# Small clipped subtractions on GpSimd, a later triangle selection, and padded tiles in a two-layer retention and delta-rule encoder

## The chip, the cores and the metric

The kernel runs on one core of one Trainium2 chip. The metric is the device time in microseconds of one execution. Three timed runs of the kernel before gave 1135.25 us as the median (1132.84, 1135.25 and 1136.71). A separate execution was profiled; the trace comes from that one.

The engines are named as in the profile: PE is the matrix engine, PEld its weight loads, DVE the vector engine, ACT the scalar engine, POOL is GpSimd, and SP issues nearly all transfers. L215 is line 215 of the kernel before.

## What is computed

Two layers, each with a token mixer and a feed-forward part, on a (256, 1024) float32 matrix. The parts that the change touches belong to the gated delta rule, which runs forwards and backwards over two chunks of 128 tokens, for eight heads:

```
h = rmsnorm(x);  one projection of h gives all mixer inputs and gates
gc   = cumsum(g) within a chunk                    # g < 0, so gc falls along the chunk
diff = gc[i] - gc[j]
dec  = exp(where(i >= j, diff, -inf))              # decays: 0 above the diagonal
A    = beta * (k k^T) * dec, strictly below the diagonal
solve (I + A) u = beta v                           # in blocks of 32, then 64, then 128
attn = (q k^T) * dec, diagonal included
o    = decayed q times the state + attn times (u - ...)
x    = x + W_out( gate_a * P_ret(retention) + gate_b * P_dn(delta rule) )
x    = x + W2( relu(rmsnorm(x) W1)^2 )
```

## The kernel before, in words

**Products.** Every large product is done in three parts, since a float32 operand is split in a high part and a low part: high times high, high times low, low times high. A weight tile of 128 x 1024 numbers (`wraw`, 512 KB) is loaded by SP, its high part `whi` is made by ACT (L180) and its low part `wlo` by DVE (L181). There are three buffers of each. Two helpers use them. `chan_pair` (L202) makes channel-major outputs: the weight block stays in the array and the 256 tokens are streamed, so each product has 256 columns (L215 to L217). `tok_chunk` (L184) makes token-major outputs: the tokens stay and 512 weight columns are streamed (L197 to L199). The streamed tokens are `hTh`/`hTl` (the transposed, normalized input), `h2h`/`h2l` for the feed-forward part, and `yrh`/`yrl`, `ydh`/`ydl` for the two merge projections. The names of the outputs in the profile: `pcd` (delta-rule inputs), `pcrq` (retention queries and keys), `parv`, `parg` (retention values and gates), `padz`, `pcga`, `pcgb` (gates), `pcpr`, `pcpd` (merge projections), `pawo` (output projection), `pcf` and `paf` (the two feed-forward products).

**Where tiles lie.** Pools are laid out one behind the other in a partition, a tile at its size. The weight buffers come first, each 4096 bytes; behind them the two halves of `x` (tag `x0`, `x1`), then `hTh0`, `hTh1`, `hTl0`, `hTl1`, then small tiles, then the tiles of the mixer, which hold `yrh` and its like. All sizes from the first weight buffer to `hTl1` are multiples of 4096 bytes (two buffers for small projections share a slot), so `hTh`, `hTl` and the weight parts begin at the same place modulo 4096.

**Decays.** For each layer, `gates_small` (L249) makes `gc`, writes its transpose to `rowd` and reads it back into the decay tiles `E` with every row repeated over the 128 partitions (L327). There are two halves of heads (`hf`), each with two directions `d`, so four pieces of 128 x 1024 numbers a layer. POOL subtracts `gc` from a whole piece (L330, a tensor of columns broadcast along the rows) and then sets everything on the wrong side of the diagonal to -1e30 (L334, an affine selection). ACT takes the exponential of a half at a time (L341), which makes those places 0. The buffers of the later block solve, `W` (L338), `D` (L498) and `DT` (L505), are set to zero by POOL.

**Delta rule.** `half_inputs` (L371) projects keys and queries of a half, passes them through a convolution of five taps (L358 to L364, on ACT and DVE) and transposes them. The sums of squares `ssq` go to POOL for a power of -0.5 (`rs`, L130 called from L395); `sA` (L404, L405) is made from it. `delta_kk` (L434) multiplies the products `ps_kk` by `sA` and `E` into `A` (L448) and by `E` alone into `E` itself (L450, the attention weights), all on DVE; then diagonal blocks of 32 go through memory to `delta_solve` (L463), which starts with X = -Gm and ones on the diagonal (L468, L469) and runs 30 steps of two DVE operations (L474, L476). X and its transpose `XT` go to memory and come back in 40 small transfers for `delta_levels` (L484; products `ps_y` L515, `ps_m` L525, `ps_mt` L532), and then follows `delta_out` (L563).

**Order.** The body is written as generators for retention and delta rule, interleaved by the string `SEQ` (L59). A scheduler then orders each engine's instructions, with priorities for weight loads and splits, and that order is fixed when the program runs: an engine whose next instruction waits does nothing else. At the start of a layer `normed` (L133) waits for POOL as well: the power `r` (L130) of the mean square is taken there, for each of the two token tiles, before DVE can scale `x` (`xn`, L145) and PE can transpose it (`pstn`, L167).

Of the kernel before, what the change touches and what calls it, by code (L numbers as in the profile page):

```python
# [8 lines left out]
F32 = mybir.dt.float32  # L9
F32R = mybir.dt.float32r  # L10
AF = mybir.ActivationFunctionType
ALU = mybir.AluOpType
AX = mybir.AxisListType

P = 128
D = 1024
S = 256
DEPTH = 2
NT = S // P
# [4 lines left out]
HH = 4  # L24
CK = 5
# [10 lines left out]
def tile_trunk(ctx, tc, x, norm1_g, w_in, conv_w, a_log, dt_bias, ret_gn_g, dn_norm_g,  # L36
# [3 lines left out]
    V, A, G, T = nc.vector, nc.scalar, nc.gpsimd, nc.tensor  # L40

    def pool(name, bufs, space=None, c=ctx):
        kw = {} if space is None else {"space": space}
        return c.enter_context(tc.tile_pool(name=name, bufs=bufs, **kw))

    cst = pool("cst", 1)
    wp = pool("wp", 3)
    hp = pool("hp", 1)
# [9 lines left out]

    SEQ = "11111011101101"  # L59

    xh = [hp.tile([P, NT, 512], F32, tag=f"x{j}", name=f"x{j}") for j in range(2)]
    cc = cst.tile([P, C_END - C_GAM], F32, tag="cc", name="cc")
    prow = sm.tile([P, 4, P], F32, tag="junk", name="prow")
    rows1, rows2, crow = prow[:16, 0], prow[:34, 1], [prow[:CK * 24, 2 + l] for l in range(DEPTH)]
# [40 lines left out]

    gT = cst.tile([P, 16], F32, tag="gT", name="gT")
    gT2 = cst.tile([P, 34], F32, tag="gT2", name="gT2")
    cw = [cst.tile([P, CK * 24], F32, tag=f"cw{l}", name=f"cw{l}") for l in range(DEPTH)]

    def columns(dst, src, n):  # L110
        ps = aux.tile([P, 512], F32, tag="aux", name="ps_g")
# [106 lines left out]
        return ps  # L218

    def halves(tag, p, nm, dt=F32R):  # L220
        return [p.tile([P, 4, S], dt, tag=f"{tag}{j}", name=f"{nm}{j}") for j in range(2)]

    hT_hi, hT_lo = None, None
    for l in range(DEPTH):
# [24 lines left out]
        def gates_small():  # L249
# [6 lines left out]
            for k in range(KT):  # L256
                a, b = hT_hi[k // 4][:, k % 4, :], hT_lo[k // 4][:, k % 4, :]
# [4 lines left out]
            with tc.high_priority(offset=300):  # L262
# [30 lines left out]
                p = s16("spp")  # L293
# [16 lines left out]
                gc = gx[:, 0]  # L310
# [12 lines left out]
            for hf in range(2):  # L323
                for d in range(2):
                    E = Es[hf][:, d]
                    for c in range(NT):
                        DQ.dma_start(  # L327
                            E[:, c], rowd[d, c, d, HH * hf:HH * hf + HH, :].partition_broadcast(P))
                    i0 = 8 * d + HH * hf
                    G.tensor_tensor(E, E, gc[:, :, i0:i0 + HH].unsqueeze(3).broadcast_to([P, NT, HH, P]),  # L330
                                    ALU.subtract)
                    ev = E.rearrange("p c h i -> p (c h) i")
                    sg = 1 if d == 0 else -1
                    G.affine_select(ev, ev, pattern=[[0, 8], [sg, P]], base=0, channel_multiplier=-sg,  # L334
                                    compare_op=ALU.is_ge, fill=-1e30)
            Ws = [dl.tile([P, 8, P], F32, tag="W", name="W", bufs=2) for hf in range(2)]
            for hf in range(2):
                G.memset(Ws[hf], 0.0)  # L338
# [95 lines left out]
        def delta_kk(hf, q):  # L434

            kq, sA = q["kq"], q["sA"]
            E = [sc["E"][hf][:, d] for d in range(2)]
            Am = [dl.tile([P, NT, HH, P], F32, tag=f"A{d}", name=f"A{d}", bufs=2) for d in range(2)]
            for c in range(NT):
                cs = slice(c * P, (c + 1) * P)  # L440
                for i in range(2):
                    ps = dps.tile([P, 2, 2, P], F32, tag="dps", name="ps_kk")
                    for e in range(2):
                        T.matmul(ps[:, e], lhsT=kq[i][:, e, 0, cs], rhs=kq[i][:, e, :, cs], start=True, stop=True)
                    for d in range(2):
                        for e in range(2):
                            h = 2 * i + e
                            V.scalar_tensor_tensor(Am[d][:, c, h, :], ps[:, e, 0, :], sA[:, d, c, h:h + 1],  # L448
                                                   E[d][:, c, h, :], ALU.mult, ALU.mult)
                        V.tensor_tensor(E[d][:, c, 2 * i:2 * i + 2, :], ps[:, :, 1, :],  # L450
                                        E[d][:, c, 2 * i:2 * i + 2, :], ALU.mult)
            adg = sm.tile([P, 16, 32], F32, tag="junk", name="adg")
            Av = [a.rearrange("p c h i -> p (c h) i") for a in Am]
            for b in range(4):
                bs = slice(32 * b, 32 * b + 32)
                A.activation(adg[bs, 0:8, :], Av[0][bs, :, bs], AF.Copy)
                V.transpose(adg[bs, 8:16, :], Av[1][bs, :, bs])
            for d, b, c in PAIRS:
                G.tensor_copy(sc["W"][hf][blk[b], :, blk[c]], Av[d][blk[b], :, blk[c]])
            DQ.dma_start(sc["gd"][64 * hf:64 * hf + 64].rearrange("(u b) (j i) -> (b j) u i", b=4, i=32), adg)  # L460
            q.update(E=E, Av=Av)

        def delta_solve():  # L463

            Gm = dl.tile([P, 32, 32], F32, tag="G", name="Gm")
            DQ.dma_start(Gm, sc["gd"].rearrange("q (j i) -> q j i", i=32))
            X = dl.tile([P, 32, 32], F32, tag="X", name="X")
            V.tensor_scalar(X, Gm, -1.0, None, ALU.mult)  # L468
            V.memset(X.rearrange("p a b -> p (a b)")[:, 0:1024:33], 1.0)  # L469
            for j in range(1, 31):  # L470
                n = 31 - j
                tm = sm.tile([P, 256], F32, tag="stm", name="stm", bufs=1)
# [319 lines left out]
        for i in range(4):  # L792
            ps = chan_pair(w_proj_dn[l][:, 256 * i:256 * (i + 1)], yTh, yTl, "pd")
            for e in range(2):
                k = 2 * (i % 2) + e
# [5 lines left out]
        xh = [hp.tile([P, NT, 512], F32, tag=f"x{j}", name=f"x{j}") for j in range(2)]  # L801
# [23 lines left out]
        for i in range(16):  # L825
            ps = chan_pair(w_ff1[l][:, 256 * i:256 * (i + 1)], hT_hi, hT_lo, "f1")
            for e in range(2):
                k = 2 * i + e
# [82 lines left out]
```

## Time and profile before

| | us |
|---|---|
| median of three timed runs | 1135.25 |
| profiled execution, its own time | 1128.0 |
| its span, first to last instruction | 1126.3 |
| PE busy | 1082.3 |
| PEld busy | 1003.9 |
| DVE busy | 765.7 |
| ACT busy | 599.5 |
| POOL busy | 195.2 |

The mean granted clock of PE is 0.982 of full speed. Busy times of PE are modelled and overlap with each other, so the spacing of the starts of products says more than the length of one. The stages in the profiled execution, by its timeline: layer 0 has its mixer first, the feed-forward products from 384 us on, and ends at 566 us; layer 1 follows in the same way. POOL begins on the decays at 63 us and at 620 us, and the block solve runs from 150 to 202 us and from 706 to 758 us.

### The profile page before, as it was taken

Reading aid. Unit: us, or ns where it says so; the run is one execution under the profiler, and the core shown is the slowest. Engines: PE = TensorE matmul, PEld = TensorE weight load, DVE = VectorE, ACT = ScalarE, POOL = GpSimd, SP = SyncE. Lnnn points to the kernel's source line nnn. Section 1 sums busy time; section 2 is a strip of 40 time slices with the busy share of each in tenths; the row PEclk is TensorE's granted clock in tenths of the full one; section 3 lists DMA queues with packets and bytes.
Section 4 is the critical chain, followed back from the end, with each engine's and each line's share of the span. In section 5 each row is a group of like instructions: output and inputs, shape, how many; then the busy total and the mean of one; then the engine's idle time right before and its main releaser. Section 6 shows DMA issues by size and latency. Waiting matters only on the chain. (4 is left out here: it accounts for less than half of the span.)

```text
span 1126.3 us, 19629 instructions
## 1 busy us (share of the span) xinstructions
PE 1082.3 (96%) x7564; PEld 1003.9 (89%) x7564; DVE 765.7 (68%) x1359; ACT 599.5 (53%) x1046; POOL 195.2 (17%) x193
## 2 busy tenths in 40 slices
PE   6988999999999999999989899999999999999997
PEld 5988888989999899988879898989999989999885
DVE  4998999646576666644468898994657566666453
ACT  5986654433364566533359865454334556555342
POOL 2065200100002043300020751001001012332000
PEclk9999999989999999999999899999999999999999
DMA  6565675453545466556556556655444565655662
GB/s 211 160 182 157 173 211 150 114 158 97 153 145 183 157 203 182 177 191 211 171 165 177 161 162 193 187 154 135 124 142 113 173 204 165 192 185 188 188 194 104
DMA packets 175759, 188.43 MB, mean 167 GB/s; under 512 B 36240, under 2 KB 137010, under 8 KB 175666
## 3 DMA queue, kind: packets, MB, share of 16 engines
q1 hardware_dynamic: 174288, 185.17, 55.0%
q10 hardware_dynamic: 1378, 2.02, 0.5%
q8 instruction: 59, 0.97, 0.4%
q14 instruction: 34, 0.28, 0.1%
HBM read 181.85 MB, written 5.31 MB: 166 GB/s over the span
## 5 line engine op out<-in xcount | busy, mean ns | idle before, releaser
L181 DVE TENSOR_TENSOR wlo<-wrawc,whi 128x1024 fp32r<-128x1024 f32 x192 | 240.7, 1254 | 117.3 <-ACT whi L180 113.3
L180 ACT ACTIVATE whi<-wrawc 128x1024 fp32r<-128x1024 f32 x192 | 202.7, 1057 | 150.0 <-PE pcpr L216 25.3
L181 DVE TENSOR_TENSOR wlo<-wraw,whi 128x1024 fp32r<-128x1024 f32 x128 | 158.2, 1236 | 111.7 <-ACT whi L180 111.6
L180 ACT ACTIVATE whi<-wraw 128x1024 fp32r<-128x1024 f32 x128 | 135.5, 1059 | 172.3 <-PE paf L199 92.0
L216 PE MATMUL pcf<-h2l,whi 128*128 128x256 f32 x512 | 143.8, 283 | 0.0
L217 PE MATMUL pcf<-h2h,wlo 128*128 128x256 f32 x512 | 143.0, 283 | 0.0
L215 PE MATMUL pcf<-h2h,whi 128*128 128x256 f32 x512 | 142.0, 284 | 0.0
L217 PE MATMUL pcd<-hTh,wlo 128*128 128x256 f32 x384 | 110.8, 292 | 0.9 <-DVE wlo L181 0.9
L215 PE MATMUL pcd<-hTh,whi 128*128 128x256 f32 x384 | 110.3, 291 | 0.0
L216 PE MATMUL pcd<-hTl,whi 128*128 128x256 f32 x384 | 109.8, 287 | 0.0
L199 PE MATMUL paf<-whi,fl 128*128 128x512 f32 x256 | 100.8, 394 | 0.0
L198 PE MATMUL paf<-wlo,fh 128*128 128x512 f32 x256 | 100.7, 394 | 0.0
L216 PEld LDWEIGHTS pcf<-h2l,whi 128*128 128x128 f32 x512 | 98.2, 192 | 0.0
L217 PEld LDWEIGHTS pcf<-h2h,wlo 128*128 128x128 f32 x512 | 98.0, 192 | 0.0
L215 PEld LDWEIGHTS pcf<-h2h,whi 128*128 128x128 f32 x512 | 97.1, 192 | 0.0
L197 PE MATMUL paf<-whi,fh 128*128 128x512 f32 x256 | 90.2, 392 | 0.0
L832 POOL TENSOR_TENSOR fz<-fz 128x256 f32<-128x256 f32 x64 | 66.6, 1042 | 117.7 <-ACT fz L831 116.7
L215 PEld LDWEIGHTS pcd<-hTh,whi 128*128 128x128 f32 x384 | 73.9, 194 | 1.1 <-issue 0.2
L217 PEld LDWEIGHTS pcd<-hTh,wlo 128*128 128x128 f32 x384 | 73.5, 193 | 1.6 <-DVE wlo L181 1.2
L216 PEld LDWEIGHTS pcd<-hTl,whi 128*128 128x128 f32 x384 | 74.1, 193 | 0.4
L363 DVE SCALAR_TENSOR_TENSOR cacc<-pcd,cw,cacc 128x255 f32<-128x255 f32 (+1 forms) x144 | 67.1, 475 | 5.7 <-ACT cac L359 4.7
L197 PEld LDWEIGHTS paf<-whi,fh 128*128 128x128 f32 x256 | 48.1, 188 | 11.0
(268 smaller groups left out, 2637.6 us busy)
## 6 DMA issues: line engine op xcount, KB each, us to landing
wrawc<-in_w_in_dram SPq DMA_DIRECT2D x96, 512.0 KB, 3.8
wrawc<-in_w_ff_dram SPq DMA_DIRECT2D x64, 512.0 KB, 3.7
wraw<-in_w_ff_dram SPq DMA_DIRECT2D x64, 512.0 KB, 3.7
wraw<-in_w_in_dram SPq DMA_DIRECT2D x48, 512.0 KB, 3.7
wrawc<-in_w_proj_ret_dram SPq DMA_DIRECT2D x16, 512.0 KB, 3.4
wrawc<-in_w_proj_dn_dram SPq DMA_DIRECT2D x16, 512.0 KB, 3.4
wraw<-in_w_out_dram SPq DMA_DIRECT2D x16, 512.0 KB, 3.7
E<-rowd SPq DMA_DIRECT2D x16, 256.0 KB, 5.3
```

The lines of the kernel that those rows point to most:

```text
L180: A.activation(hv, raw, AF.Copy)
L181: V.tensor_tensor(lv, raw, hv.bitcast(F32), ALU.subtract)
L197: T.matmul(ps[t], lhsT=a, rhs=wh[:, kk, :], start=k == 0, stop=False)
L198: T.matmul(ps[t], lhsT=a, rhs=wl[:, kk, :], start=False, stop=False)
L199: T.matmul(ps[t], lhsT=b, rhs=wh[:, kk, :], start=False, stop=k == nk - 1)
L215: T.matmul(ps[i], lhsT=wh[:, kk, c], rhs=a, start=k == 0, stop=False)
L216: T.matmul(ps[i], lhsT=wh[:, kk, c], rhs=b, start=False, stop=False)
L217: T.matmul(ps[i], lhsT=wl[:, kk, c], rhs=a, start=False, stop=k == KT - 1)
L363: V.scalar_tensor_tensor(a[:, o], ps[i][:, q], wk(k), a[:, o], ALU.mult, ALU.add)
L832: G.tensor_tensor(z2, z, z, ALU.mult)
```

## The change

Four things are edited.

- The decay subtraction is cut from pieces of 128 x 1024 to pieces of 128 x 128: for each chunk and head one `tensor_scalar` on POOL, whose scalar is a column of `gc` (one value for each partition), with a second step that takes the minimum with 0. 32 instructions a layer take the place of four.
- The selection is moved from before the exponential to the end of `delta_kk`, where it sets the wrong side of the attention product `E` to 0. Before it, the exponential there is at most 1, because of the minimum. `A` is no longer masked on the wrong side.
- In `delta_solve`, X is set to zero and its diagonal to one by POOL, and only the part above the diagonal is filled from Gm, by five small DVE operations on strided blocks.
- Three tags are padded in their second buffer: `x1` by 448 bytes, `cw1` by 96 and `hTl1` by 128 in each partition.

```
-    xh = [hp.tile([P, NT, 512], F32, tag=f"x{j}", name=f"x{j}") for j in range(2)]
+    xh = [hp.tile([P, NT * 512 + 112 * j], F32, tag=f"x{j}", name=f"x{j}")[:, :NT * 512]
+          .rearrange("p (t c) -> p t c", t=NT) for j in range(2)]
...
-    cw = [cst.tile([P, CK * 24], F32, tag=f"cw{l}", name=f"cw{l}") for l in range(DEPTH)]
+    cw = [cst.tile([P, CK * 24 + 24 * l], F32, tag=f"cw{l}", name=f"cw{l}")[:, :CK * 24] for l in range(DEPTH)]
...
-        return [p.tile([P, 4, S], dt, tag=f"{tag}{j}", name=f"{nm}{j}") for j in range(2)]
+        return [p.tile([P, 4 * S + (32 * j if tag == "hTl" else 0)], dt, tag=f"{tag}{j}", name=f"{nm}{j}")
+                [:, :4 * S].rearrange("p (k s) -> p k s", k=4) for j in range(2)]
...
-                    i0 = 8 * d + HH * hf
-                    G.tensor_tensor(E, E, gc[:, :, i0:i0 + HH].unsqueeze(3).broadcast_to([P, NT, HH, P]),
-                                    ALU.subtract)
-                    ev = E.rearrange("p c h i -> p (c h) i")
-                    sg = 1 if d == 0 else -1
-                    G.affine_select(ev, ev, pattern=[[0, 8], [sg, P]], base=0, channel_multiplier=-sg,
-                                    compare_op=ALU.is_ge, fill=-1e30)
+                    for c in range(NT):
+                        for h in range(HH):
+                            u = 8 * d + HH * hf + h
+                            G.tensor_scalar(E[:, c, h, :], E[:, c, h, :], gc[:, c, u:u + 1], 0.0,
+                                            ALU.subtract, ALU.min)
...
             DQ.dma_start(sc["gd"][64 * hf:64 * hf + 64].rearrange("(u b) (j i) -> (b j) u i", b=4, i=32), adg)
+            for d in range(2):
+                ev = E[d].rearrange("p c h i -> p (c h) i")
+                sg = 1 if d == 0 else -1
+                G.affine_select(ev, ev, pattern=[[0, 8], [sg, P]], base=0, channel_multiplier=-sg,
+                                compare_op=ALU.is_ge, fill=0.0)
...
-            V.tensor_scalar(X, Gm, -1.0, None, ALU.mult)
-            V.memset(X.rearrange("p a b -> p (a b)")[:, 0:1024:33], 1.0)
+            xf, gf = (t.rearrange("p a b -> p (a b)") for t in (X, Gm))
+            G.memset(X, 0.0)
+            G.memset(xf[:, 0:1024:33], 1.0)
+
+            for n in (16, 8, 4, 2, 1):
+                xs, gs = (bass.AP(tensor=f.tensor, offset=f.offset + n, ap=[f.ap[0], [66 * n, 16 // n], [32, n], [1, n]])
+                          for f in (xf, gf))
+                V.tensor_scalar(xs, gs, -1.0, None, ALU.mult)
```

In the layout that results, `hTh` and `hTl` begin 448 bytes behind the weight parts modulo 512 (0 before), the mixer's tiles `yrh`, `ydh`, `mTh` and layer 0's `fh`, `fl` also 448 (384 before), and layer 1's `fh`, `fl` 0 (448 before).

**The order of POOL in layer 0 from the decays to the copies into `W`.** `E` are the decay tiles, `rs` the power for the keys and queries, `ru` and `rT` the rotary steps of retention, `W` and `A` belong to the block solve. Before:

```order
19 L330 TENSOR_TENSOR E<-E,gx 128x1024 x2
20 L334 AFFINE_SELECT E<-E 128x1024
21 L330 TENSOR_TENSOR E<-E,gx 128x1024
22 L334 AFFINE_SELECT E<-E 128x1024
23 L130 TENSOR_TENSOR rs<-ssq,mh 128x16
24 L330 TENSOR_TENSOR E<-E,gx 128x1024
25 L334 AFFINE_SELECT E<-E 128x1024 x2
26 L651 TENSOR_TENSOR ru<-ru,rot 128x256 x2
27 L652 TENSOR_TENSOR rT_1059<-ru,rw 128x256 x2
```

and after (its own line numbers):

```order
20 L336 TENSOR_SCALAR E<-E,gx 128x128 x32
21 L132 TENSOR_TENSOR rs<-ssq,mh 128x16
22 L664 TENSOR_TENSOR ru<-ru,rot 128x256 x4
23 L665 TENSOR_TENSOR rT_1077<-ru,rw 128x256 x4
24 L664 TENSOR_TENSOR ru<-ru,rot 128x256 x3
25 L132 TENSOR_TENSOR rs<-ssq,mh 128x16
26 L664 TENSOR_TENSOR ru<-ru,rot 128x256
27 L665 TENSOR_TENSOR rT_1716<-ru,rw 128x256 x4
28 L461 COPY W<-A_732 32x8x32 x2
29 L466 AFFINE_SELECT E<-E 128x1024
30 L461 COPY W<-A_733 32x8x32 x2
```

All the subtractions of both halves now stand ahead of the first `rs`, the selections stand among the copies into `W`, and both `rs` come before any of them.

On DVE the step that waits for `rs` (`irk`, L398) moves with it: in layer 0 from row 119 of its order to row 136. Six more low weight parts (`wlo`), eight rotary products (`rw`) and one more convolution pair (six `cacc` of L363, two of L364, and one left of the pair before) stand ahead of it; in layer 1 it is likewise behind six more `wlo`. The exponential of half 0 on ACT stands one weight part later than before in both layers, that of half 1 four later.

**The order of PE at layer 0's block levels.** `pcga` are products of a gate, `ps_y`, `ps_m` and `ps_mt` those of the levels. Before:

```order
1210 L216 MATMUL pcga_3069<-hTl_119,whi 128x256
1211 L217 MATMUL pcga_3069<-hTh_117,wlo 128x256
1212 L515 MATMUL ps_y<-dd,W 128x32 x8
1213 L525 MATMUL ps_m<-W,DT_1463 32x32 x8
1214 L525 MATMUL ps_m<-W,DT_1464 32x32 x8
1215 L525 MATMUL ps_m<-W,DT_1489 32x32 x8
```

and after:

```order
1233 L218 MATMUL pcga_3094<-hTl_120,whi 128x256
1234 L219 MATMUL pcga_3094<-hTh_118,wlo 128x256
1235 L528 MATMUL ps_y<-dd,W 128x32 x8
1236 L538 MATMUL ps_m<-W,DT_1488 32x32 x8
1237 L538 MATMUL ps_m<-W,DT_1489 32x32 x8
1238 L538 MATMUL ps_m<-W,DT_1514 32x32 x8
```

The same small products stand behind the second half (`hTh_118`) of that gate's products, and not behind its first half: 24 products of 256 columns more are ahead of them.

**The order of POOL at the start of layer 1.** `fz` is the last square of the feed-forward part, `r` the power that the normalization waits for. Before, five rows:

```order
78 L832 TENSOR_TENSOR fz_5536<-fz 128x256
79 L338 MEMSET W 128x1024 x2
80 L498 MEMSET D_6132 128x512
81 L498 MEMSET D_6133 128x512
82 L130 TENSOR_TENSOR r_6145<-r_6145,mh 128x1
```

and after:

```order
76 L340 MEMSET W 128x1024 x2
77 L476 MEMSET X 128x1024
78 L511 MEMSET D_6157 128x512
79 L511 MEMSET D_6158 128x512
80 L132 TENSOR_TENSOR r_6170<-r_6170,mh 128x1
81 L477 MEMSET X 128x32
82 L132 TENSOR_TENSOR r_6181<-r_6181,mh 128x1
```

One more zeroing of 128 x 1024 stands ahead of the first `r`, and one of 32 numbers ahead of the second.

## The prediction

> **What bounds the kernel now.** I read the page first: busy times and the slices of the span.
>
> ```profile
> PE 1082.3 (96%) x7564; PEld 1003.9 (89%) x7564; DVE 765.7 (68%) x1359; ACT 599.5 (53%) x1046; POOL 195.2 (17%) x193
> PE   6988999999999999999989899999999999999997
> DVE  4998999646576666644468898994657566666453
> ```
>
> PE is the bound nearly everywhere. DVE is full at its side in slices 2 to 7 and again in 22 to 27, the projections of the two mixers, and there PE is not always full. The stretches (PE, PEld, DVE, ACT, POOL busy; clock; DMA share; GB/s) give the size:
>
> ```profile
> 75.00:100.00 25.00, 21.60 (x167) 20.71 (x167) 24.62 (x56) 21.39 (x45) 16.22 (x17) 1.00 0.52 147
> 225.00:250.00 25.00, 22.22 (x212) 21.48 (x209) 10.86 (x15) 8.99 (x14) 0.00 (x0) 0.80 0.54 157
> 625.00:650.00 25.00, 21.07 (x144) 20.41 (x143) 21.81 (x38) 20.06 (x43) 19.00 (x15) 0.80 0.37 109
> ```
>
> PE idles 3.4, 2.8 and 3.9 us here, and in two of them the granted clock falls as well: 0.80 over 25 us is 5 us of PE time lost, part of it idle. POOL is busiest in the first and the last, where it makes the decays. So there are three prices to find: what a product costs while PE is full, what the decays cost DVE and so PE, and what the block levels cost at 226 us.
>
> **The pads.** Start times in the timeline of PE tell the spacing. The first and last row of stretches without a break: 256-column products of layer 0's feed-forward part (51 steps), 512-column products of `parg` (9 steps):
>
> ```profile
> 429.76 0.28 PE L217 MATMUL pcf<-h2h,wlo 128*128 128x256 f32 x1
> 435.88 0.28 PE L217 MATMUL pcf<-h2h,wlo 128*128 128x256 f32 x1
> 159.74 0.39 PE L198 MATMUL parg<-wlo,hTh 128*128 128x512 f32 x1
> 161.78 0.39 PE L199 MATMUL parg<-whi,hTl 128*128 128x512 f32 x1
> ```
>
> That is 6.12/51 = 0.1200 us and 2.04/9 = 0.2267 us, both with the two operands at distance 0 modulo 512 bytes. Other distances are in the trace too; here counts in full stretches, of `pcpd` (distance 384) in layer 1, of `paf` in layer 0 (384) and in layer 1 (448):
>
> ```profile
> 890.00:916.00 26.00, 22.95 (x192) 1.00 0.57 184
> 490.00:550.00 60.00, 60.00 (x259) 1.00 0.61 199
> 1045.00:1100.00 55.00, 55.00 (x242) 1.00 0.62 191
> ```
>
> 192 `pcpd` in 22.95 us, less the 0.28 us of the last, are (22.95-0.28)/191 = 0.1187 us each. A stretch cut anywhere counts about 1.7 products of 0.39 us already running, so `paf` takes 60/257.3 = 0.2332 and 55/240.3 = 0.2289 us. Place matters, then, by one to three per cent, and not in one direction: 384 is better than 0 for 256 columns and worse for 512. No row shows 448 with 256 columns. I take 0.1187, the row of the nearest distance; the ends are 0.1212 (as much worse than 0 as 384 is better) and 0.115, the shortest steps seen in single pairs of `pcpd`:
>
> ```profile
> 895.86 0.28 PE L216 MATMUL pcpd<-ydl,whi 128*128 128x256 f32 x1
> 895.97 0.28 PE L217 MATMUL pcpd<-ydh,wlo 128*128 128x256 f32 x1
> ```
>
> Counts from the code: 1536 `pcf`, 384 `pcga`, 384 `pcgb`, all where PE is full: 2304 x 0.0013 = 3.0 us. 1152 `pcd` and 384 `pcrq` stand where DVE is nearly full as well; I count half, 1.0 us. For 512 columns: layer 0's `paf` 384 x (0.2332-0.2289) = 1.7 less; layer 1's goes from 448 to 0, 384 x 0.0022 = 0.8 less; `pawo` 192 x 0.0043 = 0.8 less; `parv`, `parg`, `padz` go from 0 to 448, 576 x 0.0022 = 1.3 more. Sum: 3.0 + 1.0 + 2.0 = 6.0 us less; the ends are about 3840 x 0.005 + 2.0 = 21 less, and 3840 x 0.0012 - 2.0 = 2.6 more. By the Trainium skill (TensorE: Matmul & The Clock Gate, Part 2, on LDWEIGHTS) PE reads the streamed and the loaded operand through two independent ports, so that loading weights takes nothing from a running product; that speaks against any effect of their distance, and this term would be 0 by it. The rows above, 0.2289 against 0.2332 us for one line of code, do not agree with it.
>
> **The decays.** POOL and DVE around them, layer 0, then layer 1, from the timelines of POOL and DVE:
>
> ```profile
> 61.64 0.41 DVE L364 TENSOR_TENSOR cacc<-cacc,cac 128x254 f32<-128x254 f32 x1
> 62.36 1.21 DVE L181 TENSOR_TENSOR wlo<-wrawc,whi 128x1024 fp32r<-128x1024 f32 x1
> 63.45 3.93 POOL L330 TENSOR_TENSOR E<-E,gx 128x1024 f32<-128x1024 f32 x2 [50.58 <-DMA E<-rowd]
> 64.00 1.62 DVE L364 TENSOR_TENSOR cacc<-cacc,cac 128x254 f32<-128x254 f32 x1
> 65.55 2.92 DVE L181 TENSOR_TENSOR wlo<-wrawc,whi 128x1024 fp32r<-128x1024 f32 x1
> 70.38 1.18 DVE L364 TENSOR_TENSOR cacc<-cacc,cac 128x254 f32<-128x254 f32 x1
> 71.49 2.10 DVE L181 TENSOR_TENSOR wlo<-wrawc,whi 128x1024 fp32r<-128x1024 f32 x1
> ...
> 619.84 1.90 POOL L330 TENSOR_TENSOR E<-E,gx 128x1024 f32<-128x1024 f32 x1 [46.29 <-DMA E<-rowd]
> 620.31 1.71 DVE L364 TENSOR_TENSOR cacc<-cacc,cac 128x254 f32<-128x254 f32 x1
> 625.66 2.10 DVE L181 TENSOR_TENSOR wlo<-wrawc,whi 128x1024 fp32r<-128x1024 f32 x1
> 630.53 1.30 DVE L364 TENSOR_TENSOR cacc<-cacc,cac 128x254 f32<-128x254 f32 x1
> 633.55 3.08 POOL L130 TENSOR_TENSOR rs<-ssq,mh 128x16 f32<-128x16 f32 x1
> 636.67 1.04 DVE L398 TENSOR_TENSOR irk<-ssq,rs 128x8 f32<-128x8 f32 x1 [2.80 <-POOL rs L130]
> ```
>
> An L364 takes 0.41 us and an L181 1.21 alone, and up to 1.71 and 2.92 while POOL works on `E`. In layer 0 that is 1.21 + 1.71 + 0.77 + 0.89 = 4.6 us of DVE time, in layer 1 1.30 + 0.89 + 0.89 = 3.1, and there DVE also waits 2.80 us for `rs`, which is queued behind `E` on POOL. The Trainium skill gives the reason (SBUF — State Buffer, Who interferes with whom): a DVE instruction with two SBUF inputs and a GpSimd one that reads SBUF shut each other out for a whole instruction. The trace agrees: no delay here exceeds one POOL instruction.
>
> So a shorter POOL instruction means a shorter delay. What one of 128 x 128 with a column takes is in no row. The nearest: a selection of 128 x 128 (timeline), and sums of two tensors of 128 x 256 (groups by line, with the busy time and the mean in ns; two DVE groups needed below stand with it, and the selections of whole pieces, shortest, median and longest):
>
> ```profile
> 2.15 0.29 POOL L92 TENSOR_SCALAR_AFFINE_SELECT ident<-ident 128x128 f32<-128x128 f32 x1
> ...
> L652 POOL TENSOR_TENSOR rT<-ru,rw 128x256 f32<-128x256 f32 x16 | 16.8, 1052 | 20.0 <-DVE rw L650 20.0
> L363 DVE SCALAR_TENSOR_TENSOR cacc<-pcd,cw,cacc 128x255 f32<-128x255 f32 (+1 forms) x144 | 67.1, 475 | 5.7 <-ACT cac L359 4.7
> L650 DVE TENSOR_TENSOR rw<-pcrq,rot 64x256 f32<-64x256 f32 x32 | 13.5, 422 | 0.7
> ...
> L334 POOL TENSOR_SCALAR_AFFINE_SELECT E<-E x8: 1083/1186/2078, 67.3 to 637.7; 128x1024 f32<-128x1024 f32 x8
> ```
>
> I take 0.40, near the first (one tensor of the same size, plus the column); ends 0.29 and 1.05, blocking included. 32 x 0.40 = 12.8 us a layer on POOL, so layer 1's `rs` runs from 632.6 to 635.7 us. DVE now needs it later: six L181, eight L650, seven L363 and two L364 are 7.3 + 3.4 + 3.3 + 0.8 = 14.8 us more ahead of `irk`, which was reached at 636.67 - 2.80 = 633.9 and is now at about 648.7 us. The 2.80 us go. Of the delays I leave a fifth (0.40 for 1.9), 1 us a layer. The four selections run later, at the end of the decay products, and delay DVE there instead: four of about 1.1 us, half of which falls on two-input instructions (my choice), 2 us a layer. Balance for DVE: layer 0 4.6 - 1 - 2 = 1.6 less, layer 1 3.1 + 2.8 - 1 - 2 = 2.9 less. Since DVE sets PE's pace there, I put them on the path: 4.5 us; ends 0 and 10, the second all that PE idles in the first and last stretch above (3.4 + 3.9) and the half of the lost clock. The decay products of half 0 move behind the rotary products, next to those of 512 columns, where one L181 covers more PE time; that hides them, and if it does not, the whole 4.5 us come back as PE waits there.
>
> **Solve and levels.** DVE's first step goes, five small ones come, POOL zeroes X early:
>
> ```profile
> L468 DVE TENSOR_SCALAR X<-Gm x2: 693/694/694, 148.1 to 704.0; 128x1024 f32<-128x1024 f32 x2
> 149.84 0.16 DVE L474 TENSOR_TENSOR stm<-Gm,X 128x30 f32<-128x30 f32 x1
> 228.74 0.66 PE L525 MATMUL ps_m<-W,DT 128*32 128x32 f32 x16 [2.39 <-DMA DT<-xtd]
> ```
>
> 0.69 us, and the setting of the diagonal behind it, against five of at least 0.16, 0.8 us: 0 on balance. At 226 us PE waits 2.39 us for the last transfers of XT. 24 products of 0.12, 2.9 us, now stand ahead of that point: 2.4 us less. I leave the slow clock that follows as it is.
>
> **The start of layer 1.** Here POOL's zeroings are on the path:
>
> ```profile
> 566.50 1.84 POOL L338 MEMSET W<- 128x1024 f32 x2 [86.58 <-PE paf L199]
> 568.28 0.99 POOL L498 MEMSET D<- 128x512 f32 x2
> 569.24 0.56 POOL L130 TENSOR_TENSOR r<-r,mh 128x1 f32<-128x1 f32 x1
> 570.57 0.41 PE L167 MATMUL pstn<-ident,xn 128*128 128x128 f32 x2 [4.13 <-DVE xn L145]
> ```
>
> `r` starts when the zeroings end, and PE waits 4.13 us for `xn` behind it. One zeroing of 128 x 1024 more (1.84/2 = 0.92) is 0.9 us more, with nothing to hide it. In layer 0 the same zeroing comes before `x` has arrived and costs nothing.
>
> **Sum.** -6.0 - 4.5 - 2.4 + 0.9 = -12.0 us on the profiled execution's 1128.0 (span 1126.3 and 1.7 around it). That execution is 0.6% below the median of the three timed runs, so I set the difference against the median: 1135.25 - 12 = 1123 us. About 0.3%, 3.4 us, is what a measurement can tell from no change.
>
> **The rivals.**
> - *Distance does nothing* (0.2): PE reads its two operands without either delaying the other, and the spread of rows comes from something else, the phase in which a stretch starts. 1135.25 - 6 = 1129 us. For it: 0.1200 holds over 51 steps as if it were a fixed price. Against: the two layers' `paf`. The Trainium skill's two ports (the section named above) would have it so.
> - *Distance does more* (0.13): 448 is as good as the best pairs, 0.115. 1135.25 - 27 = 1108 us.
> - *Slow small instructions* (0.13): each pays a long start. From 0.81 us on, 32 of them and `rs` (3.08 us) end after 648.7 us, and DVE waits at `irk` with its weight parts and convolutions queued behind, and PE for those. At 1.05 us `rs` ends at 619.84 + 33.6 + 3.08 = 656.5, 7.8 us late; as much in layer 0 and no decay gain: -6.0 - 2.4 + 0.9 + 15.6 = +8.1, 1143 us. For it: 1.05 us for the sums. Against: 0.29 us for a selection of the same size. The Trainium skill (GPSIMD Engine Reference, Instruction dispatch) has each GpSimd instruction found and called in software at a cost of tens of cycles; no run here shows that cost by itself.
> - *No room* (0.09): selections and moved decay products delay DVE as much as before and more, and the pads give nothing: 1135.25 + 0 to + 3, 1136 us.
>
> The forecast as summed has the remaining 0.45. Faster by over 0.3%, below 1131.8: forecast, distance more, and three quarters of distance nothing, 0.73. Slower, above 1138.7: slow instructions and a little of no room, 0.15. Same: 0.12. The range of 8 in 10 leaves out 0.08 below and 0.12 above: 1105 to 1141.
>
> **What would show it.** Right: `pcf` steps of 0.1187; L364 near 0.41 and no wait of `irk`; no wait of 2.4 us at `ps_m` in layer 0; PE waiting 5 us at `xn` in layer 1. Wrong: `pcf` steps of 0.120 or more; small subtractions of over 0.8 us; the clock falling at new places in the stretch from 100 to 150 us; DVE long at the copies into `W`.

## The result, and the profile after

The changed kernel takes 1124.28 us (median of 5 runs, 1123.34 to 1126.56), the kernel before in the same session 1132.84 us (5 runs, 1132.09 to 1136.71). The ratio is 0.9919, with an interval of 0.9898 to 0.9941: 9.2 us less, at least 6.7 and at most 11.6. Differences in us are worked out from the ratio, here and below; the two medians lie 8.6 us apart. The profiled execution took 1123.3 us, with a span of 1121.6.

The busy times, from the page of the changed kernel:

```profile
PE 1075.8 (96%) x7564; PEld 996.0 (89%) x7564; DVE 758.9 (68%) x1365; ACT 598.2 (53%) x1046; POOL 234.7 (21%) x253
```

PE still bounds the kernel. POOL works 39.5 us more and DVE 6.8 us less. The three stretches of the prediction, with the same columns as there:

```profile
75.00:100.00 25.00, 20.94 (x154) 20.62 (x154) 17.85 (x29) 20.32 (x36) 25.00 (x27) 0.86 0.50 146
225.00:250.00 25.00, 24.25 (x258) 23.41 (x259) 11.69 (x17) 9.39 (x16) 0.00 (x0) 0.80 0.57 164
625.00:650.00 25.00, 21.71 (x171) 20.91 (x169) 18.72 (x32) 22.34 (x43) 25.00 (x26) 0.93 0.53 149
```

In the first and the third DVE is relieved (24.62 to 17.85 us, 21.81 to 18.72), as the change intends, and POOL is full for all 25 us. PE gained little from it: it idles 4.1 and 3.3 us, where it was 3.4 and 3.9, and its granted clock (the column behind POOL's) fell from 1.00 to 0.86 in the first and rose from 0.80 to 0.93 in the third. The middle stretch has clearly less idle time, 0.75 us for 2.8.

So most of the gain lies elsewhere. Counts of PE in four stretches without a break, two in the feed-forward part's first half (`pcf`, 256 columns: the first and third rows) and two in its second half (`paf`, 512 columns), the kernel before first:

```profile
400.00:460.00 60.00, 60.00 (x502) 1.00 0.64 193
...
980.00:1020.00 40.00, 40.00 (x335) 1.00 0.59 182
```

and the changed kernel:

```profile
400.00:460.00 60.00, 60.00 (x512) 1.00 0.63 190
490.00:550.00 60.00, 60.00 (x259) 1.00 0.61 195
980.00:1020.00 40.00, 40.00 (x342) 1.00 0.61 187
1045.00:1100.00 55.00, 55.00 (x244) 1.00 0.60 195
```

A stretch cut anywhere counts some products that are already running: 0.28/0.12 = 2.3 of those with 256 columns, 1.7 of the others. A product of 256 columns took 60/499.7 = 0.1201 us before and takes 60/509.7 = 0.1177 now, in layer 1 40/339.7 = 0.1177. A product of `paf` takes 60/257.3 = 0.2332 in layer 0, as before, and 55/242.3 = 0.2270 in layer 1, where it took 0.2289. Elsewhere the step is shorter still; first and last of 35 steps of `pcrq` (timeline of PE):

```profile
75.56 0.28 PE L217 MATMUL pcrq<-hTh,whi 128*128 128x256 f32 x1
...
79.53 0.28 PE L219 MATMUL pcrq<-hTh,wlo 128*128 128x256 f32 x1
```

These are 3.97/35 = 0.1134 us each, at a granted clock of 1.00 from 75.5 to 79.6 us: the same distance of 448 bytes has two steps, 0.1134 and 0.1177. Which one a stretch takes is settled soon after it begins and then holds: in the start times of the changed kernel it changes at a break between products, and layer 0's `pcf` keep one step over 670 products.

### The profile page after: what moved, and what is told of

Read it like the earlier page. It is cut to its first block, busy times and chain, and to the rows that moved or that the text cites. A ratio compares the mean times of both kernels' runs of the same rounds, so it can differ in the third digit from the quotient of the medians.

```text
span 1121.6 us, 19699 instructions
## 1 busy us (share of the span) xinstructions
PE 1075.8 (96%) x7564; PEld 996.0 (89%) x7564; DVE 758.9 (68%) x1365; ACT 598.2 (53%) x1046; POOL 234.7 (21%) x253
## 4 chain that ended last, share of the span: by engine, by line
PE 79%; DMA 5%; DVE 5%; POOL 3%; ACT 3%; SPq 2%; issue 2%; POOLq 0%; ACTq 0%
PE pcf L219 5%; PE pcf L217 5%; PE pcf L218 5%; PE paf L201 5%; PE paf L199 5%; PE paf L200 5%; POOL E L336 2%; PE pcd L217 2%; PE pcd L218 2%; PE pcd L219 2%; DMA wrawc<-in_w_in_dram 2%; DVE wlo L183 2%; PE parg L200 1%; PE pcpd L218 1%; PE pcpd L217 1%
## 5 line engine op out<-in xcount | busy, mean ns | idle before, releaser
L183 DVE TENSOR_TENSOR wlo<-wrawc,whi 128x1024 fp32r<-128x1024 f32 x192 | 237.4, 1236 | 121.4 <-ACT whi L182 117.0
L183 DVE TENSOR_TENSOR wlo<-wraw,whi 128x1024 fp32r<-128x1024 f32 x128 | 158.2, 1236 | 109.3 <-ACT whi L182 109.2
L845 POOL TENSOR_TENSOR fz<-fz 128x256 f32<-128x256 f32 x64 | 69.0, 1079 | 111.5 <-ACT fz L844 94.1
L336 POOL TENSOR_SCALAR E<-E,gx 128x128 f32<-128x128 f32 x64 | 60.3, 961 | 96.4 <-DVE cacc L365 49.6
```

The costliest lines, as they stand in the source:

```text
L183: V.tensor_tensor(lv, raw, hv.bitcast(F32), ALU.subtract)
L336: G.tensor_scalar(E[:, c, h, :], E[:, c, h, :], gc[:, c, u:u + 1], 0.0, ALU.subtract, ALU.min)
L845: G.tensor_tensor(z2, z, z, ALU.mult)
```

## The experiments

Distances are bytes modulo 512 from the weights (`whi`, `wlo`) to the other operand, by the tiles' addresses. Ratios are against the kernel before on the same chip, with the 95% interval.

**The pads alone, and all but the pads.** The first is the kernel before with the three pads of the diff, the second the changed kernel without them.

> The kernel before with the three pads alone. Theory A (the pads bring the whole gain, and the small subtractions with the late selections cost some of it back): faster than the changed kernel, 1118 to 1122 us, 0.987 to 0.990 of before; products of 256 columns settle at 0.1178 us in the long stretches as in the changed kernel. Theory B (the two halves of the change each give about half, as predicted): 1126 to 1130 us, 0.994 to 0.997. Theory C (the pads do nothing for the time, the steps only move the waits): 1132 to 1135 us.

> The changed kernel without the three pads: small subtractions, late selections, the new first step of the solve. Theory A: as slow as before or slower, 1133 to 1138 us, 1.000 to 1.005 of before; subtractions at 0.71 us alone as in the changed kernel, products of 256 columns at 0.1200 us. Theory B: 1126 to 1130 us, 0.994 to 0.997. Theory C: the whole gain, 1124 us.

The pads alone: 1120.05 us, ratio 0.9901 (0.9881 to 0.9922), 11.2 us less. All but the pads: 1135.38 us, ratio 1.0026 (1.0008 to 1.0043), 2.9 us more. Theory A holds, and B and C fall: the pads bring the gain, and the rest gives some of it back (more on that under "What stays open"). Together they make 8.3 us less, for 9.2 measured. PE with the pads alone, in the same stretches:

```profile
400.00:460.00 60.00, 60.00 (x511) 1.00 0.62 190
...
980.00:1020.00 40.00, 40.00 (x355) 1.00 0.64 196
```

Layer 0 takes 0.1180 us a product, layer 1 40/352.7 = 0.1134: one kernel shows both steps.

**Distance or place.** One pad each on the kernel before:

```diff
-    xh = [hp.tile([P, NT, 512], F32, tag=f"x{j}", name=f"x{j}") for j in range(2)]
+    xh = [hp.tile([P, NT * 512 + 112 * j], F32, tag=f"x{j}", name=f"x{j}")[:, :NT * 512]
+          .rearrange("p (t c) -> p t c", t=NT) for j in range(2)]
```

```diff
-    cw = [cst.tile([P, CK * 24], F32, tag=f"cw{l}", name=f"cw{l}") for l in range(DEPTH)]
+    cw = [cst.tile([P, CK * 24 + 24 * l], F32, tag=f"cw{l}", name=f"cw{l}")[:, :CK * 24] for l in range(DEPTH)]
```

> The kernel before with the pad behind x1 alone: the weights stay at 128 modulo 512 bytes, the normalized inputs move to 64 (distance 448 as in the changed kernel), the other left operands to distance 320 or 384. If the distance of the two operands sets the step: pcf at 0.1178 us, and 1122 to 1128 us. If the place of the weights alone sets it: pcf at 0.1200 us and 1131 to 1135 us.

> The kernel before with the pad behind the convolution weights alone: everything behind it moves by 96 bytes, the weights to 224 modulo 512, and every distance stays as before (0, 384, 448). If the distance sets the step: pcf at 0.1200 us, and 1132 to 1135 us, as before. If the place of the weights by itself sets it: pcf at 0.1178 us and 1122 to 1128 us.

`x1` alone: 1123.18 us, 0.9922 (0.9900 to 0.9944). `cw1` alone: 1131.93 us, 1.0012 (0.9994 to 1.0029), no change. PE with the pad behind `x1`, then with the one behind `cw1`:

```profile
400.00:460.00 60.00, 60.00 (x512) 1.00 0.64 192
...
1045.00:1100.00 55.00, 55.00 (x238) 1.00 0.57 187
```

```profile
400.00:460.00 60.00, 60.00 (x502) 1.00 0.63 191
```

Moving all tiles by 96 bytes together leaves 502 products in 60 us, moving one operand against the other gives 512. The distance sets the step, not the place. (The pad behind `x1` moves all that lies behind it, `fh` too; that it is the distance of the product's own operands is seen below, where `fh` is moved alone.) The same pad makes `paf` in layer 1 slower (238 for 242, 0.2328 for 0.2289 us): it went from 448 to 384 there.

**Which distances.** The same edit with 16, 48, 64, 8 and 24 numbers in place of 112.

> The kernel before with 64 bytes behind x1: normalized inputs at distance 64 from the weights, the other left operands of 256-column products at 448, fh at 448 (layer 0) and 0 (layer 1). If any distance but 0 does: pcf settles at 0.1133 or 0.1178 us and the time is 1118 to 1125 us. If it has to be behind the weights' place by 64 to 128 bytes (320 to 448): pcf at 0.1200 us, pcpd at 0.1133 or 0.1178, and 1128 to 1132 us. paf in layer 1 at 0.2267 us in both cases.

> The kernel before with 192 bytes behind x1: normalized inputs at distance 192, the other left operands at 64, fh at 64 and 128. If any distance but 0 does: pcf and pcpd at 0.1133 or 0.1178 us, 1118 to 1125 us. If only 320 to 448 do: both at about 0.1200 us, 1131 to 1135 us. A distance at which each stretch settles at 0.1133 us would give 1112 to 1116 us.

> The kernel before with 256 bytes behind x1: normalized inputs at distance 256, half of the period, the other left operands at 128, fh at 128 and 192. If any distance but 0 does: pcf and pcpd at 0.1133 or 0.1178 us, 1118 to 1125 us. If only 320 to 448 do: both at about 0.1200 us, 1131 to 1135 us. If half the period keeps the two operands farthest apart: each stretch at 0.1133 us, 1112 to 1116 us.

> The kernel before with 32 bytes behind x1: normalized inputs at distance 32 from the weights, the other left operands at 416, fh at 416 and 480. By the runs so far the distance counts modulo 256 bytes: 0 gives 0.1200 us for a product of 256 columns, 128 gives 0.1187, 64 and 192 give 0.1133 or 0.1178. If steps of 64 bytes are all that counts: 32 acts as 0 (pcf 0.1200) and 416 as 384 (pcpd 0.1187), 1128 to 1133 us. If any place off a multiple of 128 frees the product: both at 0.1133 or 0.1178 us, 1119 to 1125 us.

> The kernel before with 96 bytes behind x1: normalized inputs at distance 96, the other left operands at 480, fh at 480 and 32. If steps of 64 bytes are all that counts: 96 acts as 64 (pcf at 0.1133 or 0.1178 us) and 480 as 448 (pcpd the same), 1120 to 1126 us. If any place off a multiple of 128 frees the product: the same here, and in the run with 32 bytes too. A place where every stretch settles at 0.1133 us would give 1112 to 1116 us.

PE of the five kernels in the order 64, 192, 256, 32, 96; of the first, `paf` of layer 0 as well, of the last the first and last of 51 steps of `pcf` (timeline of PE):

```profile
400.00:460.00 60.00, 60.00 (x512) 1.00 0.63 192
490.00:550.00 60.00, 60.00 (x264) 1.00 0.61 202
```

```profile
400.00:460.00 60.00, 60.00 (x512) 1.00 0.63 193
```

```profile
400.00:460.00 60.00, 60.00 (x502) 1.00 0.64 193
```

```profile
400.00:460.00 60.00, 60.00 (x512) 1.00 0.63 193
...
980.00:1020.00 40.00, 40.00 (x345) 1.00 0.62 192
```

```profile
429.86 0.28 PE L218 MATMUL pcf<-h2h,wlo 128*128 128x256 f32 x1
...
435.98 0.28 PE L218 MATMUL pcf<-h2h,wlo 128*128 128x256 f32 x1
```

The last two rows give 6.12/51 = 0.1200 us, the step of the kernel before. A count is good to about one product, 0.0002 us; in the start times 0, 96 and 256 all take 0.1200, and 64, 192 and 448 take 0.1178 in layer 0.

| `h2` to weights, bytes | one `pcf` product, us | time, us | ratio |
|---|---|---|---|
| 0 (before; pad behind `cw1`) | 0.1201 | 1130.99; 1131.93 | 1; 1.0012 (0.9994 to 1.0029) |
| 32 | 0.1177, layer 1 0.1167 | 1129.54 | 0.9984 (0.9966 to 1.0002) |
| 64 | 0.1177 | 1124.84 | 0.9945 (0.9920 to 0.9971) |
| 96 | 0.1200 (start times) | 1136.71 | 1.0061 (1.0038 to 1.0085) |
| 192 | 0.1177 | 1122.87 | 0.9928 (0.9907 to 0.9949) |
| 256 | 0.1201 | 1131.41 | 1.0005 (0.9987 to 1.0022) |
| 448 (pad behind `x1`) | 0.1177, layer 1 0.1134 | 1123.18 | 0.9922 (0.9900 to 0.9944) |

256 bytes act as 0, so the pattern repeats after 256 bytes, not 512, as far as these distances show: 448 is 192, and the 384 of `pcpd` is 128 (with the pad of 256 bytes `pcpd` is at 128, and by its start times it takes the 0.1187 us that it took at 384). "Any distance but 0" falls (96, 256), and so do "any place off a multiple of 128" (96) and "only 320 to 448" (64, 192). "Steps of 64 are all that counts" falls too: 32 doesn't act as 0, nor 96 as 64. Each whole time holds other distances as well, of the products with 512 columns too. With 96 bytes `paf` of layer 1 is at 32 and takes 0.2333 us by its start times, for 0.2289, which makes 1.7 us; `parv`, `parg` and `padz` are at 96 and take 0.2340 for 0.2274, which makes 3.8 us for 576 of them. That accounts for most of the 6.9 us by which this run is slower than before, although `pcf` isn't. At 448 `paf` of layer 0 takes 60/262.3 = 0.2287 us in the run with 64 bytes. No distance tried settles at 0.1134 in every stretch.

**What the small subtractions cost.** Two variants of the changed kernel, pads included. The first takes long instructions on POOL, the second keeps the small ones and puts those of half 0 on DVE:

```diff
-                    for c in range(NT):
-                        for h in range(HH):
-                            u = 8 * d + HH * hf + h
-                            G.tensor_scalar(E[:, c, h, :], E[:, c, h, :], gc[:, c, u:u + 1], 0.0,
-                                            ALU.subtract, ALU.min)
+                    i0 = 8 * d + HH * hf
+                    G.tensor_tensor(E, E, gc[:, :, i0:i0 + HH].unsqueeze(3).broadcast_to([P, NT, HH, P]),
+                                    ALU.subtract)
+                    G.tensor_scalar(E, E, 0.0, None, ALU.min)
```

```diff
-                            G.tensor_scalar(E[:, c, h, :], E[:, c, h, :], gc[:, c, u:u + 1], 0.0,
+                            (G if hf else V).tensor_scalar(E[:, c, h, :], E[:, c, h, :], gc[:, c, u:u + 1], 0.0,
                                             ALU.subtract, ALU.min)
```

> The changed kernel, its pads too, with the 32 small subtractions of a layer replaced by 4 long subtractions and 4 long clippings; selections late as in the changed kernel. Theory A1 (GpSimd's long row of small subtractions costs the time: the exponentials on ScalarE wait for it, and TensorE for the copies queued behind them): TensorE's wait of 4.0 us for kq in layer 0 and of 2.4 us at the products ps_kk in layer 1 go, and the time is that of the pads alone, 0.988 to 0.991 of before. Theory A2 (the late selections cost it, or the new solve): as the changed kernel, 0.992 to 0.994.

> The changed kernel, with the 16 small subtractions of half 0 of each layer on VectorE and the 16 of half 1 left on GpSimd. Theory A1 (GpSimd's long row of subtractions holds up the exponentials on ScalarE, TensorE's copies behind them and the products ps_kk): ScalarE's wait of 1.6 us ahead of the first exponential and TensorE's wait of 4.0 us at ps_kt behind it go, as does the wait of 2.4 us at ps_kk in layer 1; 0.988 to 0.991 of before. Theory A2 (late selections or the solve cost it): the waits at ps_kk stay and the time is 0.992 to 0.995; the 16 instructions then cost VectorE some 2 to 5 us a layer without a return.

Long pair: 1120.43 us, 0.9900 (0.9875 to 0.9925). Split: 1119.44 us, 0.9907 (0.9879 to 0.9935). First the changed kernel: the subtractions (shortest, median, longest), POOL's row of them in layer 0 and `rs` behind it, ScalarE's exponential of half 0 and the copy `kq` behind it, and PE's waits for `kq` and for the products' buffers:

```profile
L336 POOL TENSOR_SCALAR E<-E,gx x64: 702/710/1934, 62.5 to 643.5; 128x128 f32<-128x128 f32 x64
```

```profile
62.54 30.50 POOL L336 TENSOR_SCALAR E<-E,gx 128x128 f32<-128x128 f32 x32 [49.58 <-DVE cacc L365]
93.02 2.92 POOL L132 TENSOR_TENSOR rs<-ssq,mh 128x16 f32<-128x16 f32 x1
```

```profile
75.80 1.28 ACT L343 ACT_TABLE_LOAD   x1
78.66 1.91 ACT L343 ACTIVATE E<-E 128x2048 f32<-128x2048 f32 x1 [1.58 <-POOL E L336]
...
82.06 1.28 ACT L384 ACT_TABLE_LOAD   x1
83.35 0.42 ACT L384 ACTIVATE kq<-cacc 128x256 f32<-128x256 f32 x1
```

```profile
83.82 0.69 PE L386 MATMUL ps_kt<-ident,kq 128*128 128x128 f32 x2 [4.02 <-ACT kq L384]
...
657.11 1.10 PE L446 MATMUL ps_kk<-kq 128*128 128x256 f32 x4 [2.44 <-DVE E L452]
```

The chain can be read in these rows: ScalarE is ready for the exponential at 77.08 us and waits for the sixteenth subtraction; the table of the copies comes back only behind the exponential, and PE stands 4.02 us for `kq`. `rs` ends at 95.9 us. It began at 72.49 us in the kernel before:

```profile
72.49 3.87 POOL L130 TENSOR_TENSOR rs<-ssq,mh 128x16 f32<-128x16 f32 x1
```

DVE's decay products (L450) begin at 102.0 us in the changed kernel, where they began at 80.7, and PE's products `ps_kk` come in a block that waits for their buffers. `rs` isn't all of that delay: DVE's fixed order has more in front of `irk` now, and in layer 0 DVE reaches it just after `rs` has ended.

The kernel before has waits here too, at other places. Its two largest from 60 to 160 us (in total, times, longest), and then the changed kernel's largest:

```profile
PE pcrq L215 <- DVE rw L650: 2.6, 1, 2.6
PE pcrq L215 <- DVE cacc L363: 2.2, 2, 2.0
...
PE ps_kt L386 <- ACT kq L384: 4.3, 2, 4.0
```

All the waits that this view lists for PE from 60 to 160 us add up to 7.1 us before and 6.5 in the changed kernel, those from 600 to 720 us to 4.6 and 7.6. In layer 0 the change moved the waits rather than adding to them; in layer 1 it added 3.0 us.

Now the split kernel: its subtractions on DVE, `rs` on POOL, DVE's wait for it, and PE's waits at the same place:

```profile
L336 DVE TENSOR_SCALAR E<-E,gx x32: 271/278/382, 60.2 to 620.6; 128x128 f32<-128x128 f32 x32
```

```profile
80.29 2.92 POOL L132 TENSOR_TENSOR rs<-ssq,mh 128x16 f32<-128x16 f32 x1
83.25 0.71 DVE L400 TENSOR_TENSOR irk<-ssq,rs 128x8 f32<-128x8 f32 x1 [2.34 <-POOL rs L132]
...
87.76 1.21 DVE L183 TENSOR_TENSOR wlo<-wrawc,whi 128x1024 fp32r<-128x1024 f32 x1
```

```profile
85.52 0.44 PE L386 MATMUL ps_kt<-ident,kq 128*128 128x128 f32 x2 [1.25 <-ACT kq L384]
89.03 0.58 PE L219 MATMUL pcd<-hTh,wlo 128*128 128x256 f32 x1 [3.07 <-DVE wlo L183]
```

The waits for `ps_kk` are gone and that for `kq` fell to 1.25 us; a wait of 3.07 us for `wlo` came instead. It isn't DVE's sixteen extra instructions, which end at 66 us, that make it: DVE waits 2.34 us at `irk` for `rs`, which stands on POOL behind the other sixteen subtractions, and the `wlo` that PE needs comes behind `irk` and the first decay products in DVE's order. In the long pair a clipping takes 2.77 us, and the waits for `kq` are shorter, but three (in total, times, longest):

```profile
L335 POOL TENSOR_SCALAR E<-E x8: 2768/2774/3750, 66.5 to 643.9; 128x1024 f32<-128x1024 f32 x8
```

```profile
PE ps_kt L384 <- ACT kq L382: 3.8, 3, 1.9
```

PE's waits add up to 5.9 us in the long pair and 6.0 in the split kernel from 60 to 160 us, and to 4.8 and 6.3 from 600 to 720. Both runs lie where theory A1 has them, but the changed kernel's 0.9919 is inside both intervals: that the row of subtractions makes these waits is shown, that it costs those 1 to 2 us of the whole time is not.

**A better version.** The pads alone, and `fh` of layer 0 moved by 64 bytes so that it too is at distance 0:

```diff
-        fh = [ff.tile([P, 4, S], F32R, tag=f"fh{i}", name=f"fh{i}") for i in range(8)]
+        fo = 0 if last else 16
+        fh = [ff.tile([P, 4 * S + (0 if i else fo)], F32R, tag=f"fh{i}", name=f"fh{i}")
+              [:, (0 if i else fo):].rearrange("p (k s) -> p k s", k=4) for i in range(8)]
```

> The kernel before with the three pads, and 64 bytes more ahead of fh in layer 0, so that the 384 products of 512 columns of paf there stand at distance 0 from the weights instead of 448, as they do in layer 1. If distance 0 is the best place for products of 512 columns and the worst for 256: paf in layer 0 falls from 0.233 to 0.2267 us, 384 times 0.0066, 2.5 us less than the pads alone: 1116 to 1118 us, 0.986 to 0.989 of before. If the step of 512 columns comes from the layer and not from the place: paf in layer 0 stays at 0.233 us, and 0.989 to 0.991.

1115.37 us, 0.9862 (0.9842 to 0.9882): 15.6 us less than before, better than the changed kernel, whose interval it doesn't touch. PE in the stretches of `pcf` and of `paf` in layer 0:

```profile
400.00:460.00 60.00, 60.00 (x512) 1.00 0.62 191
490.00:550.00 60.00, 60.00 (x266) 1.00 0.61 193
```

60/264.3 = 0.2270 us a product for 0.2332 with the pads alone: 384 of them make 2.4 us. `pcf`, whose results become `fh`, keeps its step, so it is the distance of a product's own two operands that counts. The gain over the pads alone is 4.4 us by the two ratios, whose intervals just meet (0.9881 to 0.9882); what is beyond 2.4 us isn't explained. For 512 columns distance 0 is the best place met, for 256 columns the worst, with 96.

## Why the prediction was right, and where not

The time was right, 1123 us for 1124.28, and faster as forecast. But that the sum came out is luck, by two errors that cancel: the pads give 11.2 us (6.0 forecast), and the rest takes 2.9 us where it was to give 4.5 + 2.4 - 0.9 = 6.0.

**The pads: mechanism right, size off.** The step that failed is "I take 0.1187, the row of the nearest distance". The distances were compared modulo 512, but 256 bytes act as 0: 384 stands for 128, and isn't near 448, which stands for 192. There the step is 0.1177 in long stretches: 1536 `pcf` make 3.7 us by the counts above, where the forecast had 2.0 us. And 0.1134 us, which was set as an end for single pairs, is held over whole stretches, so a `pcrq` there gained 0.0067 us. The merge projections, 768 products that went from 384 to 448, stood in the sum with nothing; with the pads alone a `pcpd` takes 0.1134 us for 0.1187 by its start times, 2.0 us for 384 of them. Of the places with 512 columns, layer 1's `paf` came as forecast (0.2270), layer 0's did not: 0.2332 for a forecast 0.2289. At 448 both have been seen, as with 256 columns. The rival "distance does more" was half right, "distance does nothing" fell with the single pads. The Trainium skill (TensorE: Matmul & The Clock Gate, Part 2, on LDWEIGHTS) gives the streamed and the loaded operand ports of their own; by it the distance would do nothing. The counts of 502 and 512, with only distances changed, differ from it, and they decide.

**The decays: the price failed.** "I take 0.40, near the first": a subtraction of 128 x 128 with a column takes 0.71 us alone and up to 1.93, and a row of 32 fills 30.5 us, 0.95 each. That is past the 0.81 us from which the rival of slow small instructions decides. DVE was relieved as forecast. Beside POOL's small instructions L366, the former L364, keeps its 0.41 to 0.42 us (timeline of DVE, with its wait at `irk` in layer 1):

```profile
73.39 0.42 DVE L366 TENSOR_TENSOR cacc<-cacc,cac 128x254 f32<-128x254 f32 x1
...
647.75 0.70 DVE L400 TENSOR_TENSOR irk<-ssq,rs 128x8 f32<-128x8 f32 x1 [1.04 <-POOL rs L132]
```

Now POOL waits for DVE: its longest, 1.93, is 0.71 and one L183 of 1.22. The Trainium skill (SBUF — State Buffer, Who interferes with whom) has the two shut each other out for a whole instruction, and this row agrees. What the working left out is the other reader behind POOL's row: ScalarE's exponentials, with a change of table of 1.28 us on each side. `rs` it had, but behind a row of 12.8 us, not 30.5. The rival placed the wait at `irk`; DVE waited there 1.04 us in layer 1 and not in layer 0, and the longer waits stood at `kq` and `ps_kk`. In the split kernel the rival's path is there as it was told: 2.34 us at `irk`, and PE's 3.07 us for the `wlo` behind it. So its price was right, and its 15.6 us were too many.

**The levels and the start of layer 1: nearly as forecast.** PE's wait of 2.39 us for the transfers in layer 0 is gone, and 1.26 us ahead of `ps_y` are new; with the shorter ones PE waits 1.8 us at these levels, where it waited 3.3, so 1.5 of the 2.4 us came. This is the row, and then those of POOL and PE at the start of layer 1:

```profile
225.22 2.68 PE L528 MATMUL ps_y<-dd,W 128*128 128x32 f32 x16 [1.26 <-issue]
```

```profile
559.93 1.84 POOL L340 MEMSET W<- 128x1024 f32 x2 [86.95 <-PE paf L201]
561.71 0.95 POOL L476 MEMSET X<- 128x1024 f32 x1
...
563.56 0.55 POOL L132 TENSOR_TENSOR r<-r,mh 128x1 f32<-128x1 f32 x1
```

```profile
564.78 2.03 PE L169 MATMUL pstn<-ident,xn 128*128 128x128 f32 x7 [4.91 <-DVE xn L147]
```

4.91 us for 4.13, 0.8 more for a zeroing of 0.95: 0.9 was forecast.

**What stays open.** The 2.9 us of all but the pads (0.9 to 4.9) are not settled term by term. In the start times of the same products, the kernel without pads against the one before, layer 0's decays give 0.3 us and its levels 1.1; the start of layer 1 costs 0.8, its projections and decays 1.5, and its levels 3.2. But the last term is the granted clock, which differs by as much between profiled executions of kernels that should not differ there. PE in the levels of layer 1 (the clock is the column behind the count) in the kernel before, without the pads, with the pad behind `cw1`, whose instructions and distances are those of before, in the changed kernel, and with the pads alone:

```profile
770.00:800.00 30.00, 27.81 (x282) 0.89 0.56 142
```

```profile
770.00:800.00 30.00, 27.29 (x242) 0.77 0.55 140
```

```profile
770.00:800.00 30.00, 28.32 (x230) 0.68 0.53 137
```

```profile
770.00:800.00 30.00, 27.62 (x249) 0.72 0.52 133
```

```profile
770.00:800.00 30.00, 26.40 (x216) 0.60 0.48 138
```

0.21 of 30 us, between the first and the third, is 6.3 us. The profiled execution of before had the mild case and that of the changed kernel lost 0.17 of 30 us, 5.1 us, more; without this difference the two profiled executions, 4.7 us apart, would lie about as far from each other as the medians, 8.6, or somewhat farther. Without the last term the rest costs about 1 us, where a gain of 6 was forecast.

The clock of whole runs says that this is more than the luck of one profile. The 12 runs without the pads had a mean granted clock of 0.972 to 0.978, 0.976 on average; the 23 runs of the kernel before beside them 0.976 to 0.987, 0.981 on average; and the 12 with the pad behind `cw1` 0.980 on average. Over the 73 runs of the kernel before that stand beside the experiments, a clock lower by 0.001 goes with about 0.7 us more. As an estimate from that, the 0.005 of clock are worth about 3.5 us, all of the 2.9: the rest of the change would then cost its time through the clock, and next to nothing at an equal one. With the pads this isn't seen: the changed kernel and the pads alone have nearly the same clock (0.976 and 0.977), and their ratios of 0.9919 and 0.9901 have intervals that overlap. What lowers the clock was not found. The pads alone lose by it as well: in their profiled execution the products are 7.1 us ahead of the kernel before at the first `ps_y` of layer 1 and 0.5 us behind at its last `pcga`, with a clock of 0.60 between for 0.89, and 8.4 us ahead at the end. So the shorter steps give more than the 11.2 us, and the clock takes part of it back.

## What to carry to other kernels

When PE is full, count its products in an unbroken stretch and see whether the step changes with where the two operands lie to each other; a pad of 64 bytes can be worth more than a rearranged engine, and it has to be tried by product width, since what is best for one is worst for another. Before a few long instructions are cut into many small ones, price one small one by a row of its own kind, and list who is queued behind the whole row, also on other engines. A sum that comes out right is not a sum of right terms: the two halves of a change have to be run apart.

## What was not expected of the hardware

- The step of a product depends on the distance of its two operands, and distances 256 bytes apart act alike. For 256 columns it is 0.1200 us at 0, 96 and 256, 0.1187 at 128 and 384, and 0.1178 or 0.1134 at 64, 192 and 448; for 512 columns 0.2267 to 0.2274 at 0 and 0.2289 to 0.2340 elsewhere (start times of unbroken stretches).
- At one distance there are two steps, 0.1178 and 0.1134 us, and a stretch keeps the one that it falls into. With the pads alone, layer 0 had the first and layer 1 the second. What chooses was not found.
- A subtraction with a column of 128 x 128 takes 0.71 us on GpSimd and 0.28 on VectorE, and a clipping of 128 x 1024 takes 2.77 us on GpSimd, longer than a sum of two tensors of that size (1.90).
